# A two-layer trunk on one core: modulation vectors, block sums and the ends of its two MLPs

## The chip, the cores and the metric

The kernel runs on one core of one Trainium2 chip. The metric is the device time of one execution in microseconds (us). Before the change three runs gave 3522.86, 3525.76 and 3529.64 us; the median is 3525.76 us.

## The reference, cut to what matters

The reference is one inference step of a trunk with two layers. Each layer is a mixer followed by an MLP, both between RMS norms, with shift, scale and gate vectors that come from a conditioning vector. The change touches only the MLPs and the modulation vectors:

```python
def sq_relu_mlp(h, w_up, w_down):
    return jnp.square(jax.nn.relu(h @ w_up)) @ w_down
...
    for l in range(DEPTH):
        sh1p, sc1p, g1p, sh2p, sc2p, g2p = modulation(c_ctx[None, :], w_ada[l], b_ada[l])
        sh1s, sc1s, g1s, sh2s, sc2s, g2s = modulation(c, w_ada[l], b_ada[l])
        ...                                   # mixer of the layer: yp, ys
        xp = xp + g1p * rmsnorm(yp, norm_g[l, 1])
        xs = xs + g1s * rmsnorm(ys, norm_g[l, 1])
        hp = rmsnorm(xp, norm_g[l, 2]) * (1.0 + sc2p) + sh2p
        hs = rmsnorm(xs, norm_g[l, 2]) * (1.0 + sc2s) + sh2s
        xp = xp + g2p * rmsnorm(sq_relu_mlp(hp, w_up[l], w_down[l]), norm_g[l, 3])
        xs = xs + g2s * rmsnorm(sq_relu_mlp(hs, w_up[l], w_down[l]), norm_g[l, 3])
```

There are ten tiles of 128 rows, 1024 columns wide; the MLP goes up to 4096 columns and back. One modulation vector, written (l, j) here, is a product of two conditioning rows with a 1024 x 1024 block of w_ada.

## The kernel before, in words

All products are float32 in effect: each operand is split into a high and a low part (split: a cast on ScalarE, L198, and a subtraction on VectorE, L199), and each product is three matmuls (L193 to L195). Engine names are those of the profile: PE is TensorE, DVE is VectorE, ACT is ScalarE, POOL is GpSimd, SP is SyncE, which here issues loads in the order of its queue.

`mlp` runs twice, for layers 0 and 1. Its **up part** goes over 16 column blocks p. The first two are plain products. The other 14 use a block scheme with seven products instead of eight, for which sums of blocks of the weights are needed (s1 to s4, four additions on POOL, L543 to L546, in `units`) and the products are combined on DVE (L593, L614, L619 to L625). Then `close_x` rectifies and squares (L464 on ACT, L466 on DVE), forms four sums of hidden blocks (L469 to L479) and stores seven pieces in DRAM by POOL's queue (L462). A scheduler orders these instructions.

The **down part** is written out in order (manual_schedule). It goes over seven names of products, (1, 5, 6, 7, 4, 2, 3), eight pairs k each, 56 in all; a pair is 30 matmuls into five PSUM banks. While pair k is multiplied, `make` splits the operands of pair k + 2, and SP loads the hidden pieces of pair k + 5 into tiles sa and sb. After eight pairs `take` moves the five banks out. Row tiles that are finished go through `close`: sum of squares on ACT (L898), rsqrt on POOL (L204), multiply by rsqrt and gate G (L912) and add x (L913) on DVE, then for the next stage another square, another rsqrt, and a scaling (L927). `closes` advances three of these generators by turns. After the first MLP the next mixer follows: `modulate` transposes the tiles (tp) and four `kv_product` stages multiply them into PSUM (mmo).

`ada_steps` makes a modulation vector, in one of two ways. On PE, w_ada is the operand of 32-row matmuls (L265). On DVE (acc), pieces of 128 x 256 are multiplied by the conditioning values and summed (L287, L289), the sum is transposed and reduced into adaR (L295, L296), and small matmuls (adac, L300) fold the four blocks. Loads are issued in the step that uses them (L248). The first MLP's up part makes (0,5), (1,0) and (1,1), its down part (1,2), (1,3) and (1,4), one step after each pair from k = 2; the second MLP's up part makes (1,5). All seven are made on DVE before the change.

Of the kernel before, what the change touches and what calls it, by code (L numbers as in the profile page):

```python
# [9 lines left out]
F32 = mybir.dt.float32  # L10
# [100 lines left out]
class Net:  # L111
# [122 lines left out]

    def ada_steps(self, l, j, raw, pp, ptag="mm", pbufs=None, acc=None):

# [39 lines left out]
        if acc:  # L276
            R = self.const.tile([P, 4, KD, 2], F32, tag="adaR", name="adaR")
        for n in range(4 if acc else 0):
            y = acc().rearrange("p (s f) -> p s f", s=2)
            k = 0  # L280
            while k < KD:
                for k, w in load(k, n * 256, 256):
                    for s in range(2):
                        c = self.cs[:, k, s:s + 1]
                        E = nc.gpsimd if s in AE else nc.vector
                        if k == 0:
                            E.tensor_scalar(y[:, s], w, c, None, ALU.mult)  # L287
                        else:
                            E.scalar_tensor_tensor(y[:, s], w, c, y[:, s], ALU.mult, ALU.add)  # L289
                k += 1  # L290
                if k % AY == 0 and (k < KD or AZ):
                    yield
            for s in range(2):
                z = raw()[:, 0:256]
                nc.vector.transpose(z, y[:, s])  # L295
                nc.vector.tensor_reduce(R[:, :, 2 * n:2 * n + 2, s].rearrange("p b k -> p k b"), z.rearrange("p (k b c) -> p k b c", k=2, b=4), AX.X, ALU.add)  # L296
        if acc:
# [79 lines left out]
    def mlp(self, l, h, stage, late, fills, odd=None):  # L377
# [30 lines left out]
        def make(k):  # L408

            m, v = divmod(k, 8)  # L410
            n = names[m]
            tag = (("hh1", "hl1", "hh0")[k % 3]) if m < LASTP else ("hh1", "hl1")[k % 2]
# [39 lines left out]
        with self.pool("mu", 1) as up:  # L452
# [8 lines left out]
            def close_x(p, X):  # L461
                store = lambda i, z: nc.gpsimd.dma_start(hd[p, i], z)  # L462
                for c in range(2):
                    nc.scalar.activation(X[0, c], X[0, c], AF.Square)  # L464
                for c in range(2):
                    V.scalar_tensor_tensor(X[1, c], X[1, c], 0.0, X[1, c], ALU.max, ALU.mult)  # L466
                store(2, X[0, 1])
# [65 lines left out]
            def units():  # L533
                ring = cycle([(i, q) for i in range(3) for q in "hl"][:5])
                load_up(NS)
                for p in range(NS, NP):
                    a11, a21 = [raws[p][0][:, :, c * P:(c + 1) * P] for c in range(2)]
                    a12, a22 = [raws[p][1][:, :, c * P:(c + 1) * P] for c in range(2)]
                    s = [self.slot(3, q, F32).rearrange("p (i k f) -> p i k f", i=2, k=4) for q in "hl"]
                    s1, s2, s3, s4 = [s[i // 2][:, i % 2] for i in range(4)]  # L540
                    for j, u in enumerate((a11, a12, a21, a22, s4, s2, s3, s1)):
                        if j == 1:
                            Gp.tensor_tensor(s1, a21, a22, add)  # L543
                            Gp.tensor_tensor(s2, s1, a11, sub)
                            Gp.tensor_tensor(s4, a12, s2, sub)
                            Gp.tensor_tensor(s3, a11, a21, sub)  # L546
                        if j == 5 and p + 1 < NP:
# [26 lines left out]
            araw = cycle("hl")  # L574
            steps = (_ for f in fills[0] for _ in self.ada_steps(*f, lambda: self.slot(4, next(araw), F32), pp, "tp", None, lambda: self.slot(2, "l", F32)[:, :512]))
            T1, T2, T3 = [[T[i, k] for k in range(4)] for i in (1, 2, 3)]
# [62 lines left out]
        with self.pool("my") as yp, self.pool("md") as dp, self.tc.manual_schedule(engines=IN_ORDER):  # L639
# [12 lines left out]
            at = {5: (0, 1), 6: (1, 1), 3: (1, 1)}  # L652

            def traw():
                if flow:
# [8 lines left out]
            with ExitStack() as es:  # L664
# [3 lines left out]
                def mul(k, whole=None):  # L668
# [12 lines left out]
                    if whole is not None:  # L681
                        self.gemm(bank[m, whole], L(whole), lambda u: Tu[u], range(2), False, True)
                        return
# [21 lines left out]

                def pair(k):
                    m, v = divmod(k, 8)
                    mul(k)
                    if k + 2 < NK:
# [8 lines left out]
                with self.pool("mu2") as u2:  # L718
                    U = [u2.tile([P, 512], F32, name=f"u2{i}") for i in range(5)]
                    steps = (_ for f in fills[1] for _ in self.ada_steps(*f, lambda: self.act.tile([P, 256], F32, tag="hl2", name="ada_w"), pd, "b", 8, lambda: u2.tile([P, 512], F32, tag="ada_y", name="ada_y")))  # L720
# [4 lines left out]
                    for _ in steps:  # L725
                        pass
                with self.pool("ms", 2) as sp:
                    tmp = lambda: sp.tile([P, 512], F32, tag="tmp", name="tmp", bufs=3)
                    st = lambda: sp.tile([P, 512], F32, tag="st", name="kvw_raw", bufs=2)
# [18 lines left out]
                    for k in range(32, NK - 1):  # L748
                        pair(k)
                        if k == 41:  # L750
                            G.extend(self.slot(6, q, F32) for q in "hl")
                            self.load_G(l, 1, G)
                        closes(k - 43, 0, 5)
                        if k > 49:
                            go(M0, 2)
                        if k > 51:
                            go(wt)
                    for i in range(5):
                        mul(NK - 1, i)
                        take(LASTP, i)  # L760
                        closes(5 + i, 5, 10)
                        if i == 0:
                            go(M0, 8)
                            go(wt)
                    es.close()
                    self.open[self.ps_at] = self.pool("ps", 2, psum=True)
                    pp = self.pp = self.open[self.ps_at].__enter__()
                    if odd:
                        M2 = self.modulate(2, z, nxt, out, tmp, pp)
                        go(wt)  # L770
                        odd.kv_product(0)
# [7 lines left out]
                    else:  # L779
                        closes(10, 5, 10)  # L780
                        closes(11, 5, 10)
                    for it in f:
# [102 lines left out]
    def load_x(self, stage, ts, xs):  # L885
        for t, x in zip(ts, xs):
            self.nc.sync.dma_start(x, self.x_in(stage, t))

    def close(self, ts, y, mid, z, zt, stage, G, xs, late, sp, junk, nxt, padd=()):
# [1628 lines left out]
def build(ctx, tc, a, o, k):  # L2518
# [6 lines left out]
    d = Odd(net)  # L2525
    h, late = net.mlp(0, h, 1, late, (((0, 5), (1, 0), (1, 1)), ((1, 2), (1, 3), (1, 4))), d)
    d.run(late)
# [31 lines left out]
```

## Time and profile before

| | |
|---|---|
| median of three runs | 3525.76 us |
| profiled execution, its own time | 3527.33 us |
| its span | 3525.2 us |
| mean granted clock of TensorE | 0.967 |
| busy share of PE, DVE, ACT, POOL | 92%, 66%, 44%, 22% |
| DMA over the span | 123 GB/s |

The profiled execution is a further run; its span goes from its first to its last instruction. Busy shares are means over stages that differ, so the stages are looked at one by one: the first MLP's up part ends at about 1345 us with its down part from there to about 1808 us; the second MLP's up part runs to about 3150 us and its down part from there to the end. PEclk is the clock that was granted to TensorE as a share of full speed.

### The profile page before, as it was taken

The numbers are of one execution on the slowest core, as the hardware profiler recorded it, in microseconds if no ns is written. First come the engines' busy times: TensorE is split into PE (matmuls) and PEld (weight loads), VectorE is DVE, ScalarE is ACT, GpSimd is POOL, SyncE is SP. The second block draws the span as 40 slices with busy tenths as digits, with TensorE's granted clock in tenths as the row PEclk, the third lists the DMA queues.
The fourth block names the chain that finished last, engine by engine and source line by source line (L and its number), as shares of the span: only waits on it lengthen the run. The fifth ranks groups of instructions, "written<-read, shape, count | busy, mean of one in ns | idle before, by whom it ended". The sixth has DMA issues, their size and how long they took to land. (4 is left out here: it accounts for less than half of the span.)

```text
span 3525.2 us, 50186 instructions
## 1 busy us (share of the span) xinstructions
PE 3255.6 (92%) x17957; PEld 2657.2 (75%) x17957; DVE 2326.5 (66%) x4310; ACT 1555.8 (44%) x3697; POOL 758.7 (22%) x1084
## 2 busy tenths in 40 slices
PE   7899898979989999788979999999999899999997
PEld 4788778858877788666758876666678788888886
DVE  4666766663699967887555365666655986666665
ACT  4444544443533333323455456555555333344443
POOL 2323332321133330001211033000001333310112
PEclk9999999989999999999989999999999999999999
DMA  6333343273344536554432221000143343455444
GB/s 208 79 101 110 98 134 96 81 216 123 107 152 167 185 137 219 175 176 143 155 118 63 78 73 34 4 8 8 35 157 118 122 170 118 149 185 174 149 141 168
DMA packets 329959, 435.27 MB, mean 123 GB/s; under 512 B 30157, under 2 KB 231213, under 8 KB 329709
## 3 DMA queue, kind: packets, MB, share of 16 engines
q1 hardware_dynamic: 307116, 343.18, 31.6%
q0 software_dynamic: 22592, 88.89, 6.7%
q8 instruction: 141, 2.31, 0.3%
q14 instruction: 110, 0.89, 0.1%
HBM read 309.55 MB, written 122.43 MB: 123 GB/s over the span
## 5 line engine op out<-in xcount | busy, mean ns | idle before, releaser
L193 PE MATMUL y<-oph 128*128 128x512 f32 x896 | 352.3, 393 | 14.3 <-ACT y L694 4.9
L194 PE MATMUL y<-opl,oph 128*128 128x512 f32 x896 | 351.7, 393 | 0.0
L195 PE MATMUL y<-oph,opl 128*128 128x512 f32 x896 | 351.6, 392 | 0.0
L199 DVE TENSOR_TENSOR opl<-sa,oph 128x512 fp32r<-128x512 f32 x216 | 158.8, 735 | 202.7 <-ACT oph L198 202.4
L198 ACT CAST oph<-sa 128x512 fp32r<-128x512 f32 x216 | 133.7, 619 | 252.2 <-PE y L194 186.1
L193 PEld LDWEIGHTS y<-oph 128*128 128x128 f32 x896 | 170.3, 190 | 51.6 <-ACT y L694 5.4
L194 PEld LDWEIGHTS y<-opl,oph 128*128 128x128 f32 x896 | 170.1, 190 | 35.8
L195 PEld LDWEIGHTS y<-oph,opl 128*128 128x128 f32 x896 | 170.0, 190 | 35.6
L193 PE MATMUL mmf<-hh,wf_hi 128*128 128x512 f32 (+1 forms) x384 | 152.6, 397 | 0.0
L1007 DVE SCALAR_TENSOR_TENSOR u<-pre,cw,u 128x510 f32<-128x510 f32 (+2 forms) x192 | 144.1, 759 | 9.7 <-ACT u L1005 8.5
L462 POOL DMA_DIRECT2D hd<-x x96 | 52.6, 548 | 452.7 <-ACT x L464 296.3
L193 PE MATMUL mmt<-wt_hi,hh 128*128 128x256 f32 x480 | 148.9, 310 | 0.0
L204 POOL TENSOR_SCALAR rs_v<-ss 128x1 f32<-128x1 f32 x90 | 27.7, 307 | 540.7 <-ACT junk L898 392.7
L195 PE MATMUL mmf<-hh,wf_lo 128*128 128x512 f32 (+1 forms) x384 | 139.9, 364 | 0.0
L194 PE MATMUL mmf<-hl,wf_hi 128*128 128x512 f32 (+1 forms) x384 | 139.4, 363 | 0.0
L194 PE MATMUL mmt<-wt_lo,hh 128*128 128x256 f32 x480 | 136.8, 285 | 0.0
L195 PE MATMUL mmt<-wt_hi,hl 128*128 128x256 f32 x480 | 136.8, 285 | 0.0
L193 PE MATMUL o<-wh,hh 128*128 128x512 f32 x280 | 113.1, 404 | 0.0
L195 PE MATMUL o<-wh,hl 128*128 128x512 f32 x280 | 110.5, 395 | 0.0
L194 PE MATMUL o<-wl,hh 128*128 128x512 f32 x280 | 110.1, 393 | 0.0
L1935 PE MATMUL pom<-PTm,mla_h 128*64 128x256 f32 x336 | 106.5, 402 | 2.4 <-DVE ob L1947 2.0
L1935 PE MATMUL pom<-PTm,mla_l 128*64 128x256 f32 x336 | 107.0, 403 | 0.0
(1064 smaller groups left out, 10368.4 us busy)
## 6 DMA issues: line engine op xcount, KB each, us to landing
sa<-hd SPq DMA_DIRECT2D x108, 512.0 KB
hd<-s POOLq DMA_DIRECT2D x128, 320.0 KB, 2.6
hd<-x POOLq DMA_DIRECT2D x96, 320.0 KB, 2.7
wh<-in_w_down SPq DMA_DIRECT2D x40, 512.0 KB
wl<-in_w_down SPq DMA_DIRECT2D x40, 512.0 KB
w_raw<-in_w_ada SPq DMA_DIRECT2D x32, 512.0 KB
wh<-in_w_up SPq DMA_DIRECT2D x30, 512.0 KB
wl<-in_w_up SPq DMA_DIRECT2D x30, 512.0 KB
```

The lines of the kernel that those rows point to most:

```text
L193: mm(ps, lh, rh, start=first and j == 0, stop=False)
L194: mm(ps, lh, rl, start=False, stop=False)
L195: mm(ps, ll, rh, start=False, stop=last and j == n - 1)
L198: self.nc.scalar.copy(hi, raw)
L199: self.nc.vector.tensor_tensor(lo, raw, hi.bitcast(F32), ALU.subtract)
L204: nc.gpsimd.tensor_scalar(v, ss, scale, eps, ALU.mult, ALU.add)
L462: store = lambda i, z: nc.gpsimd.dma_start(hd[p, i], z)
L1007: nc.vector.scalar_tensor_tensor(us, pre[:, i:i + e - a], cw[:, b, j + i:j + i + 1], us, ALU.mult, ALU.add)
L1935: self.nc.tensor.matmul(self.po[64 * b:64 * b + 64, 0], self.odd.Vm[(0 if self.big else 10) + 2 * i + b][:, 64 * self.h:64 * self.h + 64], ...
```

## The change: what it does

In `ada_steps` a vector folded on DVE now loads its pieces a given number of steps ahead (`ahead`), has a step of its own before the last reduction's matmul and one more after it, and takes the tile of the transpose from a ring named by the caller (`turn`). In the up parts the pieces are 512 columns wide instead of 256. The block sums of the weights go from POOL to DVE, between the splits. `close_x` rectifies and squares on ACT alone. In the first MLP's down part only (1,2) and (1,3) are folded, at a rate that `pace` gives; (1,4) is made on PE in `more`, between the kv products after the MLP. `closes` goes through its tiles in the other order. In the second MLP the last two row blocks of the last product are multiplied bank by bank, and five tiles end in a new generator, `close_last`.

```diff
         if acc:
             R = self.const.tile([P, 4, KD, 2], F32, tag="adaR", name="adaR")
-        for n in range(4 if acc else 0):
-            y = acc().rearrange("p (s f) -> p s f", s=2)
...
+            y = acc()
+            f = y.shape[1] // 2
+            todo, got = [(n, k) for n in range(D // f) for k in range(KD)], []
+            def fetch(c):
+                while len(got) <= c and todo:
+                    n, k = todo[0]
+                    ws = load(k, n * f, f)
+                    del todo[:len(ws)]
+                    got.extend(ws)
...
+                for k in range(KD):
+                    fetch(c + 2 * ahead - 1 if c % 2 == 0 else c)
+                    w = got[c][1]
...
+                    if c % 2 == 0:
+                        fetch(c + 2 * ahead - 1)
+                        yield
+                m = f // P
+                for s in range(2):
+                    z = turn()[:, :f]
+                    nc.vector.transpose(z, y[:, s])
+                    nc.vector.tensor_reduce(R[:, :, m * n:m * n + m, s].rearrange("p b k -> p k b"), ...)
+                yield
+            yield
...
                 for c in range(2):
-                    V.scalar_tensor_tensor(X[1, c], X[1, c], 0.0, X[1, c], ALU.max, ALU.mult)
+                    nc.scalar.activation(X[1, c], X[1, c], AF.Square)
...
+                    adds = {0: (s1, a21, a22, add), 1: (s2, s1, a11, sub), 2: (s4, a12, s2, sub), 3: (s3, a11, a21, sub)}
                     for j, u in enumerate((a11, a12, a21, a22, s4, s2, s3, s1)):
-                        if j == 1:
-                            Gp.tensor_tensor(s1, a21, a22, add)
...
+                        if j in adds:
+                            V.tensor_tensor(*adds[j])
...
+            pace = lambda k: (2, *[int(k % 8 in (0, 2, 3, 5, 6))] * 4, 2 * (k < 44), 0)[k // 8]
...
                     for k in range(32):
                         pair(k)
-                        if k > 1:
-                            next(steps, None)
+                        go(steps, pace(k))
...
+                    if last:
+                        for n, t in enumerate(H[0]):
+                            x = (2, "h"), (2, "l"), (3, "h"), (3, "l"), (0, "h")
+                            f[5 + n] = self.close_last(t, y[t], G, lambda n=n: self.slot(*x[n], F32), stage, sp, junk, tmp)
                     def closes(w, lo, hi):
-                        for n in (w - 2, w - 1, w):
+                        for n in (w, w - 1, w - 2):
...
+                    ends = [NK - 2, NK - 1] if last else [NK - 1]
...
                     for i in range(5):
-                        mul(NK - 1, i)
+                        for k in ends:
+                            mul(k, i)
                         take(LASTP, i)
+                        if last:
+                            go(f[5 + i])
+                            if i:
+                                go(f[4 + i])
+                            continue
                         closes(5 + i, 5, 10)
                         if i == 0:
                             go(M0, 8)
-                            go(wt)
+                        go(wt)
...
+                        more = (_ for f in fills[2] for _ in self.ada_steps(*f, st, pp, "tp"))
...
                         odd.kv_product(1)
                         go(M2, 4)
                         closes(11, 5, 10)
+                        go(more, 5)
                         odd.kv_product(2)
+                        go(more, 5)
                         odd.kv_product(3)
...
+                        go(more, 9)
...
+    def close_last(self, t, y, G, x, stage, sp, junk, tmp):
...
+        nc.scalar.activation(junk()[:, :512], h[0], AF.Square, accum_out=ss[:, 0:1])
+        V.tensor_tensor(h[0], h[0], g[0], ALU.mult)
+        yield
...
+        r = self.rsqrt(sp, ss[:, 0:1], 1, 1.0 / D)
+        for q, a in zip(self.halves(x), (h[0], u)):
+            V.scalar_tensor_tensor(q, a, r, q, ALU.mult, ALU.add)
+        nc.sync.dma_start(self.x_out(stage, t), x)
```

The order of instructions shows three places.

On DVE, where the first MLP's last product is taken out of its banks, before the change (y4 to y9 are row tiles, xr tiles of x, wl6 and wh6 the gates):

```order
L704 TENSOR_TENSOR y4_13313<-y4_13313,y3_16726 128x512
L912 SCALAR_TENSOR_TENSOR y9_13312<-y9_13312,rs_r_17220,wl6_16310 128x1024
L913 TENSOR_TENSOR xr_17215<-y9_13312,xr_17215 128x1024
L704 TENSOR_TENSOR y5_13314<-y5_13314,y3_16727 128x512
L927 TENSOR_SCALAR y9_13312<-xr_17215,rs_r_17257 128x1024
L912 SCALAR_TENSOR_TENSOR y4_13313<-y4_13313,rs_r_17246,wh6_16309 128x1024
L913 TENSOR_TENSOR xr_17241<-y4_13313,xr_17241 128x1024
L704 TENSOR_TENSOR y6_13315<-y6_13315,y3_16728 128x512
```

The same place after the change:

```order
L724 TENSOR_TENSOR y4_13203<-y4_13203,y3_16452 128x512
L970 SCALAR_TENSOR_TENSOR y9_13202<-y9_13202,rs_r_16946,wl6_16020 128x1024
L971 TENSOR_TENSOR xr_16941<-y9_13202,xr_16941 128x1024
L199 TENSOR_TENSOR wl1_16976<-xr_16930,wh1_16975 128x2x416
L724 TENSOR_TENSOR y5_13204<-y5_13204,y3_16453 128x512
L970 SCALAR_TENSOR_TENSOR y4_13203<-y4_13203,rs_r_16968,wh6_16019 128x1024
L971 TENSOR_TENSOR xr_16963<-y4_13203,xr_16963 128x1024
L985 TENSOR_SCALAR y9_13202<-xr_16941,rs_r_17000 128x1024
L724 TENSOR_TENSOR y6_13205<-y6_13205,y3_16454 128x512
```

The scaling of a tile (L927, now L985) stood ahead of the next tile's multiply and add and stands behind them now; the last split of the mixer's weights (L199, wl1) has moved in between.

On PE, where the third kv product begins, before the change (tp are transposes, mmo the kv product; the first block of the product is shown):

```order
L195 MATMUL mmo<-wh_17333,hl_7_16929 128x416
...
L332 MATMUL tp<-ident,y_13317 128x128
L332 MATMUL tp<-ident,y_13312 128x128
L193 MATMUL mmo<-wh_17160,hh_0_16914 128x416
L194 MATMUL mmo<-wl_17161,hh_0_16914 128x416
```

The same place after the change, through the start of the fourth:

```order
L349 MATMUL tp<-ident,y_13207 128x128
L349 MATMUL tp<-ident,y_13202 128x128
L265 MATMUL ada_17202<-kvw_raw,cs 32x512 x8
L193 MATMUL mmo<-wh_16886,hh_0_16640 128x416
...
L195 MATMUL mmo<-wh_16975,hl_7_16655 128x416
L274 MATMUL adac<-selc,kvw_raw 128x2 x4
L265 MATMUL ada_17261<-kvw_raw,cs 32x512 x8
L193 MATMUL mmo<-wh_16886,hh_0_16640 128x416
```

Eight matmuls of vector (1,4) now stand ahead of each of the last two kv products, with their loads behind them in SP's queue.

On DVE in the first MLP's up part the additions that POOL made (L543 to L546) are new; after the change a stretch reads (L303 is the fold, L564 the block sums):

```order
L564 TENSOR_TENSOR wh3_10553<-wh5_10461,wl5_10463 128x512
L303 SCALAR_TENSOR_TENSOR wl2_10363<-wh4_10538,cs_92,wl2_10363 128x512
L564 TENSOR_TENSOR wh3_10553<-wh3_10553,wh5_10461 128x512
L303 SCALAR_TENSOR_TENSOR wl2_10363<-wh4_10538,cs_92,wl2_10363 128x512 x2
L199 TENSOR_TENSOR wh2_10556<-wh5_10461,wh2_10556 128x512
L303 SCALAR_TENSOR_TENSOR wl2_10363<-wh4_10538,cs_92,wl2_10363 128x512
L303 SCALAR_TENSOR_TENSOR wl2_10363<-wl4_10593,cs_92,wl2_10363 128x512 x2
L199 TENSOR_TENSOR wh0_10573<-wl5_10463,wh0_10573 128x512
```

The sums stand singly between folds and splits.

## Rows read from the trace of the kernel before

**Rows 1.** The page, part 1: busy time, share of the span, instructions.

```profile
PE 3255.6 (92%) x17957; PEld 2657.2 (75%) x17957; DVE 2326.5 (66%) x4310; ACT 1555.8 (44%) x3697; POOL 758.7 (22%) x1084
```

**Rows 2.** Table of stretches: window, us, busy PE, PEld, DVE, ACT, POOL, PEclk, DMA, GB/s.

```profile
985.00:1286.00 301.00, 280.56 (x1448) 236.44 (x1449) 269.57 (x470) 100.28 (x188) 105.38 (x120) 0.98 0.47 166
1375.00:1650.00 275.00, 225.86 (x967) 183.35 (x966) 223.20 (x435) 85.12 (x169) 26.17 (x20) 0.91 0.51 158
2730.00:2860.00 130.00, 115.42 (x603) 98.08 (x602) 118.83 (x198) 42.70 (x83) 42.87 (x44) 0.95 0.41 143
2900.00:3100.00 200.00, 200.00 (x1054) 170.91 (x1053) 124.92 (x168) 71.07 (x136) 71.15 (x88) 1.00 0.37 133
3150.00:3490.00 340.00, 340.00 (x1502) 281.53 (x1501) 215.60 (x313) 140.33 (x270) 46.76 (x35) 1.00 0.51 160
1808.00:1859.00 51.00, 26.25 (x114) 23.75 (x114) 25.34 (x53) 21.43 (x50) 9.90 (x24) 0.73 0.31 108
```

**Rows 3.** Waits of PE, 1345 to 1660 us: total us, times, longest.

```profile
PE adac L300 <- DVE adaR L296: 37.4, 3, 15.0
```

**Rows 4.** Waits of PE, 940 to 1345 us.

```profile
PE p L193 <- DVE x L619: 10.7, 6, 3.9
```

**Rows 5.** Waits of PE, 1660 to 1900 us.

```profile
PE mmo L193 <- ACT wh L198: 11.9, 1, 11.9
```

**Rows 6.** Timeline of DVE, 1815 to 1826 us: start, us, instruction, [idle before, releaser].

```profile
1816.40 0.68 DVE L704 TENSOR_TENSOR y<-y,y 128x512 f32<-128x512 f32 x1
1820.63 0.76 DVE L927 TENSOR_SCALAR wh<-xr,rs_r 128x1024 f32<-128x1024 f32 x1 [3.55 <-POOL rs_r L205]
1821.30 1.28 DVE L912 SCALAR_TENSOR_TENSOR y<-y,rs_r,wh 128x1024 f32<-128x1024 f32 x1
1822.62 1.23 DVE L913 TENSOR_TENSOR xr<-y,xr 128x1024 f32<-128x1024 f32 x1
1823.76 0.68 DVE L704 TENSOR_TENSOR y<-y,y 128x512 f32<-128x512 f32 x1
```

**Rows 7.** Timeline of PE and DVE, the end of the span.

```profile
3506.88 0.39 PE L195 MATMUL y<-oph,opl 128*128 128x512 f32 x1
...
3519.43 1.23 DVE L913 TENSOR_TENSOR xr<-y,xr 128x1024 f32<-128x1024 f32 x1 [0.79 <-DMA xr<-xres]
```

**Rows 8.** The chain that ended last, in order of time: start, us, what.

```profile
1898.02 3.75 DMA w_raw<-in_w_in_odd
...
3514.04 5.31 DMA xr<-xres
```

**Rows 9.** Timeline of DVE, 1014 to 1046 us.

```profile
1034.09 0.68 DVE L621 TENSOR_TENSOR x<-x,p 128x512 f32<-128x512 f32 x1
1034.69 0.69 DVE L199 TENSOR_TENSOR wl<-wh,wl 128x512 fp32r<-128x512 f32 x1
```

**Rows 10.** Groups on DVE by form, 2932 to 3082.5 us: busy, mean ns, idle before.

```profile
L199 DVE TENSOR_TENSOR wh<-wh,wh 128x512 fp32r<-128x512 f32 x13 | 14.2, 1092 | 9.4 <-ACT wh L198 8.8
L199 DVE TENSOR_TENSOR wl<-wh,wl 128x512 fp32r<-128x512 f32 x11 | 11.7, 1065 | 9.1 <-ACT wl L198 8.8
L199 DVE TENSOR_TENSOR wh<-wl,wh 128x512 fp32r<-128x512 f32 x16 | 11.0, 690 | 10.4 <-ACT wh L198 10.4
L466 DVE SCALAR_TENSOR_TENSOR x<-x 128x640 f32<-128x640 f32 x12 | 9.3, 819 | 0.0
```

**Rows 11.** Groups on DVE by form, 985 to 1239 us.

```profile
L289 DVE SCALAR_TENSOR_TENSOR wl<-wh,cs,wl 128x256 f32<-128x256 f32 x82 | 42.2, 578 | 0.0
```

**Rows 12.** Timeline of SP's queue and DVE, 1384 to 1398 us.

```profile
1384.73 3.78 SPq L248 DMA_DIRECT2D ada_w<-in_w_ada  x8
...
1388.77 0.62 DVE L287 TENSOR_SCALAR ada_y<-ada_w,cs 128x256 f32<-128x256 f32 x2 [2.86 <-DMA ada_w<-in_w_ada]
...
1394.42 3.25 DVE L289 SCALAR_TENSOR_TENSOR ada_y<-ada_w,cs,ada_y 128x256 f32<-128x256 f32 x8
```

**Rows 13.** Instructions of L265: duration in ns, minimum/median/maximum.

```profile
L265 PE MATMUL ada<-w_raw,cs x128: 592/617/1063, 7.7 to 785.5; 128*32 128x512 f32 x128
```

More of the change, by code (lines that the diff above doesn't have):

```diff
@@ L233, in ada, with ada_steps @@
             pass
-    def ada_steps(self, l, j, raw, pp, ptag="mm", pbufs=None, acc=None):
+    def ada_steps(self, l, j, raw, pp, ptag="mm", pbufs=None, acc=None, turn=None, ahead=1):
         nc = self.nc
@@ L277, in ada_steps @@
             R = self.const.tile([P, 4, KD, 2], F32, tag="adaR", name="adaR")
-        for n in range(4 if acc else 0):
-            y = acc().rearrange("p (s f) -> p s f", s=2)
-            k = 0
-            while k < KD:
-                for k, w in load(k, n * 256, 256):
+        if acc:
+            y = acc()
[7 more added lines that the diff above has]
+                    got.extend(ws)
+            c = 0
+            for n in range(D // f):
+                y = (acc() if n else y).rearrange("p (s f) -> p s f", s=2)
+                for k in range(KD):
+                    fetch(c + 2 * ahead - 1 if c % 2 == 0 else c)
+                    w = got[c][1]
+                    got[c] = None
+                    c += 1
@@ L283, in ada_steps @@
                     for s in range(2):
-                        c = self.cs[:, k, s:s + 1]
-                        E = nc.gpsimd if s in AE else nc.vector
+                        v = self.cs[:, k, s:s + 1]
                         if k == 0:
-                            E.tensor_scalar(y[:, s], w, c, None, ALU.mult)
+                            nc.vector.tensor_scalar(y[:, s], w, v, None, ALU.mult)
                         else:
-                            E.scalar_tensor_tensor(y[:, s], w, c, y[:, s], ALU.mult, ALU.add)
@@ L290, in ada_steps @@
[L290 to L296, printed above, removed]
+                            nc.vector.scalar_tensor_tensor(y[:, s], w, v, y[:, s], ALU.mult, ALU.add)
+                    if c % 2 == 0:
+                        fetch(c + 2 * ahead - 1)
+                        yield
@@ L297, in ada_steps @@
+                m = f // P
+                for s in range(2):
+                    z = turn()[:, :f]
+                    nc.vector.transpose(z, y[:, s])
+                    nc.vector.tensor_reduce(R[:, :, m * n:m * n + m, s].rearrange("p b k -> p k b"), z.rearrange("p (k b c) -> p k b c", k=m, b=4), AX.X, ALU.add)
+                yield
+            yield
         if acc:
@@ L411, in make @@
             n = names[m]
-            tag = (("hh1", "hl1", "hh0")[k % 3]) if m < LASTP else ("hh1", "hl1")[k % 2]
+            tag = (("hh1", "hl1", "hh0")[k % 3]) if m < LASTP or last else ("hh1", "hl1")[k % 2]
             t = lambda name: self.act.tile([P, 512], F32R, tag=tag, name=name)
@@ L574, in mlp @@
             araw = cycle("hl")
-            steps = (_ for f in fills[0] for _ in self.ada_steps(*f, lambda: self.slot(4, next(araw), F32), pp, "tp", None, lambda: self.slot(2, "l", F32)[:, :512]))
+            steps = (_ for f in fills[0] for _ in self.ada_steps(*f, lambda: self.slot(4, next(araw), F32), pp, "tp", None, lambda: self.slot(2, "l", F32), lambda: sx()[:, :512], 1))
             T1, T2, T3 = [[T[i, k] for k in range(4)] for i in (1, 2, 3)]
@@ L704, in take, with pair @@
                         V.tensor_tensor(z, z, ps, add)
-                def pair(k):
+                def pair(k, skip=False):
                     m, v = divmod(k, 8)
-                    mul(k)
+                    if not skip:
+                        mul(k)
                     if k + 2 < NK:
@@ L747, in mlp @@
                         wt = odd.kv_weights(self.order, lambda i: [self.slot(4, "hl"[i], F32)] if i < 2 else [st(), st()] if i < 3 else [xr()])
-                    for k in range(32, NK - 1):
+                    ends = [NK - 2, NK - 1] if last else [NK - 1]
+                    for k in range(32, ends[0]):
                         pair(k)
+                        go(steps, pace(k))
+                        if k == 44:
+                            go(steps, 99)
                         if k == 41:
@@ L887, in load_x @@
             self.nc.sync.dma_start(x, self.x_in(stage, t))
+    def close_last(self, t, y, G, x, stage, sp, junk, tmp):
+        nc, V = self.nc, self.nc.vector
+        h, g = self.halves(y), self.halves(G[t // 8])
+        ss = sp.tile([P, 2], F32, tag="ssl", name="ssl", bufs=5)
+        x = x()
+        self.load_x(stage, (t,), (x,))
+        nc.scalar.activation(junk()[:, :512], h[0], AF.Square, accum_out=ss[:, 0:1])
+        V.tensor_tensor(h[0], h[0], g[0], ALU.mult)
+        yield
+        nc.scalar.activation(junk()[:, :512], h[1], AF.Square, accum_out=ss[:, 1:2])
+        u = tmp()
+        V.tensor_tensor(u, h[1], g[1], ALU.mult)
+        yield
+        nc.gpsimd.tensor_tensor(ss[:, 0:1], ss[:, 0:1], ss[:, 1:2], ALU.add)
+        r = self.rsqrt(sp, ss[:, 0:1], 1, 1.0 / D)
+        for q, a in zip(self.halves(x), (h[0], u)):
+            V.scalar_tensor_tensor(q, a, r, q, ALU.mult, ALU.add)
+        nc.sync.dma_start(self.x_out(stage, t), x)
+        yield
     def close(self, ts, y, mid, z, zt, stage, G, xs, late, sp, junk, nxt, padd=()):
```

23 lines of the change are left out of this document (11 added, 12 removed).

## The prediction

> **What bounds the kernel now.** I read the page first: TensorE (PE) is busy 92% of the span, no other engine over 66% [rows 1]. So a microsecond counts only where PE stands still or runs at its lower clock, and the change works inside the two MLPs. I then asked for their stretches [rows 2]. Two need no help: the up part of the second MLP once its modulation vector is done (2900 to 3100 us: PE busy throughout, 1054 matmuls in 200 us, 5.27 a us) and its down part (1502 in 340 us, 4.42 a us). Against these rates the stretches in which modulation vectors are folded on VectorE (DVE) fall behind: 985 to 1286 us makes 1448 matmuls, worth 274.8 us, so 26.2 are lost; 1375 to 1650 makes 967, worth 218.9, so 56.1 are lost; 2730 to 2860 makes 603, worth 114.4, so 15.6 are lost. In all three DVE is busy 81 to 91%, in the clean ones 62 and 63%. The waits name the same culprit: in the first MLP's down part PE waits 37.4 us in only three places, for the last block reduction (adaR, L296) before the small matmul adac, which stands in PE's queue close behind it [rows 3]; in the up part it waits for DVE's sums [rows 4]. Then the two ends. From 1808 to 1859 us PE does 114 matmuls with its clock at 0.73 [rows 2]; 11.9 us of that is one wait for a weight cast [rows 5]. And 17.9 us lie between the last matmul (3506.88 + 0.39 [rows 7]) and the end of the span.
>
> **Up parts (block sums to DVE, rectify and square to ACT, wider and prefetched folds).** One pass p over a column block is 132 matmuls, 25.0 us at 5.27 a us. In the clean stretch DVE needs 124.92 / 200 x 25.0 = 15.6 us of it [rows 2]. Added: four sums; a 128x512 tensor_tensor follows the one before it by 0.60 us [rows 9], so 2.4 us. Removed: two 128x640 operations of L466, 9.3 us for 12 [rows 10], so 1.55. A third part is not in the diff: the splits that fall beside POOL's sums take 1092 and 1065 ns, the others 690 [rows 10]. In six passes 24 of 48 are slow ones, 4 a pass, and 4 x 0.39 = 1.6 us goes if POOL's arithmetic goes. Net -0.7: 14.9 us. A fold step was eight operations of 128x256 at 42.2 / 82 = 0.51 us [rows 11], and a transpose and a reduce that I count like two more: 5.1 us, 15.4 for three steps a pass, with the base 31.0 us of 25.0. Now a step is four operations of 128x512, priced at 0.60 like the sums, and less than one transpose or reduce: 4.7 x 0.60 = 2.8, three of them 8.5 a pass, 23.4 of 25.0 us with the base. DVE just keeps up. ACT takes four operations a pass for the two that DVE loses; at the 0.78 us of those it gains 3 us on a busy share of 71.07 / 200 = 36% [rows 2]: hidden. I leave 5 us of the 26.2 and 3.5 of the 15.6, since the folds' transposes now take tiles from the ring of the stored sums and so wait for stores: gains 21 and 12. Bounds: nothing gained to all of it, 0 to 42 together.
>
> **Down part of the first MLP.** A pair k is 30 matmuls, 6.8 us. DVE's own work in it is four splits at 0.60 and a half-width one, mostly with two subtractions: 2.7 to 3.9 us. Eight fold operations take 3.25 us [rows 12], the fold's transposes and reduces, counted alike, 0.8: 6.7 to 8.0 us for the pair's 6.8; on top DVE waits for loads that are issued only when they are needed (2.86 us [rows 12]). So DVE runs late and the three adac matmuls pay. After: one of the three vectors leaves, loads run three steps ahead, and pace sets two half-size steps a pair for k < 8 (2.7 + 3.25 + 0.7 = 6.7 us, level with PE), then five in eight pairs (3.9 + 1.2 = 5.1 us), so DVE is on time; and two empty steps stand between the last reduction and adac. The 37.4 us go, and with them the clock's fall to 0.91 [rows 2]. What is late next is the first eight pairs and the takes of full banks; I leave 8 of 56.1: gain 48. Bounds: 10 (waits stay, clock and takes improve) to 56.
>
> **End of the first MLP.** Two edits of opposite sign. Reordered closes: DVE now does multiply and add of the tile one back before it scales the tile two back. Before, a round was add, two squares on ACT, two rsqrts on POOL, scale and multiply in series, and takes are 7.4 us apart (1816.40 and 1823.76 [rows 6]). Now the longest work on one engine is take 0.68 + multiply 1.28 + add 1.23 + scale 0.76 = 3.95 us a round, unless the x loads (5.31 us for 512 KB [rows 8]) hold it. kv product 0 starts after the fourth take: some 5 us after the last matmul instead of 9 (1816.40 + 0.68 against 1808); the last weights' cast stands before the closes, so the 11.9 us go too. Against it: vector (1,4) now runs on PE here, 16 matmuls at 0.617 us [rows 13] = 9.9 us, their weights in 16 loads of 256 KB through two tiles. PE is in order: a load from the third on waits for the matmul that frees its tile, and kv products 2 and 3 stand behind them. A weight load of the next stage took 3.75 us [rows 8], so two tiles cost 3.75 + 0.62 + 0.1 = 4.5 us; three such rounds in the first half, four in the second. After the last matmul: kv 0 at +5, about 6 us (half clock at first), transposes that wait for ACT, kv 1 to +19.5, transposes to +22, first half to +38 (three small loads stand ahead in the queue), kv 2 to +44, second half to +61, kv 3 to +67. Before, the stage took 51 us. So it costs 15. Bounds: loads hidden, all PE work in a row (5 + four products at 4.6 + 5 + 9.9 = +38), a gain of 13; no overlap at all (14 x 4.4 + 35 = +97), a cost of 45. I keep 15, from the 3.75 us row.
>
> The Trainium skill ("DMA: Bandwidth & Descriptors", Anatomy of one DMA) fits a transfer of the gpsimd path as 2.0 us and its bytes at 436 GB/s: an estimate of 2.6 us for 256 KB, by which the seven rounds would be 8 us shorter and the sum 8 us lower. No row here shows a lone 256 KB load on SP's queue.
>
> **End of the kernel.** The last two row blocks of the last product are now multiplied bank by bank, the first half of each tile is squared and scaled before that, and x is loaded early, so the 5.31 us wait for it [rows 8] goes. What stays after the last matmul: take 0.68, multiply and add in one pass of 1.28 [rows 6], landing 4.5 (3525.2 less 3519.43 + 1.23 [rows 7]); between them half a square, its sum and rsqrt, which I bound by 2 and 5 us and put at 3.5: 10 of 17.9. Gain 8, bounds 6 and 9.5.
>
> **Sum.** 21 + 48 + 12 + 8 - 15 = 74. The profiled execution took 3527.33 us (span 3525.2), 1.6 more than the median of 3525.76: 3527.3 - 74 = 3453, as a median 3452 us.
>
> **Rivals.**
> 1. DVE stays the bound in the up parts: the sums' time is not given back by quicker splits. For it: DVE is 90% busy from 985 to 1286. Against: the slow splits [rows 10]. The gains 21 and 12 go, and 0.9 us in each of 11 folding passes comes on top: 3452 + 33 + 10 = 3495. The Trainium skill ("Perfetto Trace Analysis", Optimizing Scalar/DVE Operations) advises the opposite move, off DVE when it is saturated, GpSimd included, though it doubts that it helps between these two; the slow splits bear out the doubt. Chance 0.10.
> 2. The PE vector is hidden: loads land during the kv products and the quicker closes show in full, +38 instead of +67: 3452 - 28 = 3424. For it: DMA is 31% busy there [rows 2]. Against: two tiles only. 0.12.
> 3. The adac waits stay, since DVE is still late at k < 8 and after: 3452 + 37 = 3489. 0.06.
> 4. Slower: SP's queue. SP's loads go out in order; a fold's load waits until DVE has used its tile, and the loads sa of later pairs stand behind it. If DVE falls over three pairs (20 us) back, sa's lead is used up, and each of 32 pairs with a step runs step 1.9, load 5.3, cast 0.6, splits 3.4 in series: 11.2 for 6.8 us, 141 us in place of the gain of 48: 3452 + 48 + 141 = 3641. Before, eight fold loads at once already stood there (3.78 us of issue [rows 12]) without that. 0.04.
>
> **How the numbers follow.** The forecast holds 0.65, the rivals 0.32, anything else 0.03. Range 3424 to 3490: the likeliest case alone (3430 to 3475), rivals 2 and 3; it leaves out 1, 4 and the far bound of the end. About 0.2% (7 us) is what a measurement of this kernel can tell from no change: faster 0.94, same 0.02, slower 0.04.
>
> **What would show it.** Right: no wait of PE for adaR over 1 us; over 5.1 matmuls a us in the first up part; splits beside the sums at 0.69 us; takes of the first MLP's last product about 4 us apart; PE waiting 20 to 30 us for L265's loads between the kv products; the last matmul 10 us before the end. Wrong: DVE over 95% busy in the up parts, sa's loads late, or PE waits at L265 under 10 us.

## The result and the profile after

The changed kernel took 3443.56 us (median of four runs, 3439.49 to 3445.69), the kernel before 3524.31 beside it: a ratio of 0.9767, 95% interval 0.975 to 0.9784. The forecast was 3452. The profiled execution has a span of 3441.7 us, 83.5 less than before. Part 1 of its page, as [rows 1]:

```profile
PE 3250.1 (94%) x17997; PEld 2645.0 (77%) x17997; DVE 2236.0 (65%) x4130; ACT 1635.7 (48%) x3829; POOL 603.7 (18%) x977
```

The stretches after, with the columns of [rows 2]: first MLP's up part, its down part, the kv products after it, second MLP's up part.

```profile
982.00:1263.00 281.00, 275.20 (x1441) 233.58 (x1440) 241.30 (x383) 126.91 (x233) 41.21 (x77) 0.99 0.52 175
1351.00:1531.00 180.00, 180.00 (x802) 148.72 (x801) 148.40 (x272) 73.42 (x141) 11.60 (x10) 1.00 0.63 194
...
1733.00:1797.00 64.00, 46.79 (x157) 26.91 (x157) 14.22 (x22) 14.71 (x31) 7.52 (x14) 0.74 0.38 119
2668.00:2784.00 116.00, 111.21 (x598) 95.23 (x597) 100.63 (x160) 51.94 (x98) 15.68 (x29) 1.00 0.48 163
```

The up part now makes 1441 matmuls in 281 us, 5.13 a us, where [rows 2] had 4.81; the second stretch has no gap. The waits of PE, from 912 to 1333 us and from 1333 to 1690 us, the longest of each, answer to [rows 3, 4]; adaR is not among them:

```profile
PE p L193 <- DVE x L637: 4.1, 5, 1.6
```

```profile
PE y L193 <- DVE y L724: 1.7, 1, 1.7
```

At the first MLP's end (1690 to 1800 us) the wait of [rows 5] is gone and one for the loads of vector (1,4) is new. The wait of kv product 0 for its take stays:

```profile
PE ada L265 <- DMA kvw_raw<-in_w_ada: 12.7, 9, 2.8
PE mmo L193 <- DVE y L724: 10.2, 1, 10.2
```

In the kernel before (1660 to 1900 us) it was:

```profile
PE mmo L193 <- DVE y L704: 9.2, 1, 9.2
```

The timeline of PE shows the first half of vector (1,4). Each row is four records, two for each of L265's f32 matmuls (the code issues 16, the trace has 32 records):

```profile
1751.72 1.65 PE L265 MATMUL ada<-kvw_raw,cs 128*32 128x512 f32 x4 [0.47 <-ACT tmp L355]
1756.16 2.61 PE L265 MATMUL ada<-kvw_raw,cs 128*32 128x512 f32 x4 [2.79 <-DMA kvw_raw<-in_w_ada]
1760.88 2.54 PE L265 MATMUL ada<-kvw_raw,cs 128*32 128x512 f32 x4 [2.10 <-DMA kvw_raw<-in_w_ada]
1765.62 2.50 PE L265 MATMUL ada<-kvw_raw,cs 128*32 128x512 f32 x4 [2.21 <-DMA kvw_raw<-in_w_ada]
```

On DVE the takes (L724) of the last product, [rows 6] before, stand 5.3 to 6.1 us apart; a weight split and a wait for rsqrt lie between them:

```profile
1720.59 0.68 DVE L724 TENSOR_TENSOR y<-y,y 128x512 f32<-128x512 f32 x1
1721.19 1.28 DVE L970 SCALAR_TENSOR_TENSOR y<-y,rs_r,wl 128x1024 f32<-128x1024 f32 x1
...
1725.77 1.03 DVE L199 TENSOR_TENSOR wl<-xr,wh 128x832 fp32r<-128x832 f32 x1 [2.05 <-ACT wh L198]
1726.71 0.68 DVE L724 TENSOR_TENSOR y<-y,y 128x512 f32<-128x512 f32 x1
...
1731.35 0.75 DVE L985 TENSOR_SCALAR y<-xr,rs_r 128x1024 f32<-128x1024 f32 x1 [1.50 <-POOL rs_r L205]
1732.02 0.68 DVE L724 TENSOR_TENSOR y<-y,y 128x512 f32<-128x512 f32 x1
```

The end of the span, [rows 7] before: 11.3 us lie behind the last matmul (3441.7 less 3429.99 + 0.39), not 17.9. L943 is the multiply and add of `close_last`.

```profile
3429.99 0.39 PE L195 MATMUL y<-oph,opl 128*128 128x512 f32 x1
...
3434.54 0.74 DVE L943 SCALAR_TENSOR_TENSOR wh<-tmp,rs_r,wh 128x512 f32<-128x512 f32 x1
```

The table gives all kernels by stage, in us. The stages are cut by names of tiles, in each kernel's one profile: at the first matmul of ups (the plain products of an up part), of y (the banks of a down part) and of qaps (the product behind the kv products), and at the last of y; "end 0" runs from the first MLP's last matmul to qaps, behind the kv products. Not shown: the mixer between (727 to 730) and the second down part (381 in all).

| kernel | median | ratio to before | start | up 0 | down 0 | end 0 | up 1 | end 1 |
|---|---|---|---|---|---|---|---|---|
| before | 3524.31 | | 907.8 | 447.0 | 453.3 | 159.3 | 431.8 | 18.0 |
| changed | 3443.56 | 0.975-0.9784 | 912.3 | 420.9 | 389.5 | 180.5 | 417.6 | 11.4 |
| c0 | 3432.65 | 0.9737-0.9767 | 898.1 | 421.5 | 389.4 | 179.9 | 418.0 | 11.4 |
| e1 | 3462.58 | 0.9815-0.9846 | 905.9 | 434.4 | 389.4 | 179.8 | 428.5 | 11.4 |
| e2 | 3434.77 | 0.9738-0.9774 | 903.0 | 426.5 | 389.4 | 179.8 | 420.8 | 11.4 |
| e3 | 3407.24 | 0.9647-0.9688 | 906.4 | 423.0 | 394.5 | 146.4 | 418.2 | 11.4 |
| e4 | 3399.82 | 0.9635-0.967 | 906.2 | 420.1 | 389.4 | 146.4 | 417.6 | 11.4 |
| e5 | 3403.06 | 0.9657-0.9686 | 905.0 | 421.1 | 395.5 | 147.3 | 418.7 | 11.3 |
| e6 | 3413.08 | 0.9658-0.9715 | 901.9 | 423.7 | 402.0 | 143.1 | 419.4 | 11.4 |
| e9 | 3399.93 | 0.9645-0.9674 | 896.5 | 422.9 | 389.4 | 148.3 | 418.0 | 11.4 |
| e10 | 3406.41 | 0.9646-0.9683 | 905.0 | 423.9 | 394.8 | 146.6 | 418.0 | 11.4 |
| e11 | 3406.11 | 0.9657-0.9686 | 904.9 | 419.2 | 396.9 | 146.0 | 418.4 | 11.4 |
| e12 | 3409.78 | 0.9669-0.9704 | 901.6 | 424.2 | 393.2 | 153.7 | 416.4 | 11.4 |
| e13 | 3406.87 | 0.9659-0.9689 | 907.7 | 422.9 | 389.4 | 150.6 | 417.5 | 11.4 |

### The profile page after: what moved, and what is told of

Read it like the earlier page. It is cut to its first block, busy times and chain, and to the rows that moved or that the text cites. A ratio compares the mean times of both kernels' runs of the same rounds, so it can differ in the third digit from the quotient of the medians.

```text
span 3441.7 us, 50028 instructions
## 1 busy us (share of the span) xinstructions
PE 3250.1 (94%) x17997; PEld 2645.0 (77%) x17997; DVE 2236.0 (65%) x4130; ACT 1635.7 (48%) x3829; POOL 603.7 (18%) x977
## 5 line engine op out<-in xcount | busy, mean ns | idle before, releaser
L199 DVE TENSOR_TENSOR opl<-sa,oph 128x512 fp32r<-128x512 f32 x216 | 158.8, 735 | 167.2 <-ACT oph L198 166.9
L405 ACT ACTIVATE x<-x 128x512 f32<-128x512 f32 x112 | 70.3, 628 | 78.7 <-DVE x L638 60.5
```

The source lines that it names most:

```text
L199: self.nc.vector.tensor_tensor(lo, raw, hi.bitcast(F32), ALU.subtract)
L405: relu = lambda o, i: nc.scalar.activation(o, i, AF.Relu)
```

## The experiments

**c0, the changed kernel again.**

> The changed kernel once more, as the mark for the others of this batch. The stage ahead of the first MLP, whose code is the same in all kernels, took 907.8 us in the profile of before and 912.3 in that of after, but 903.0 to 906.4 in the three variants; if that is chance, it comes out near 906 here, and the time at 3437 to 3443 us. Rival: the change itself makes that stage longer (912 again).

The rival is out: the start came out at 898.1 us, and over all profiles of the same code it lies between 896.5 and 912.3. It scatters more than I expected, and the time came out lower than I expected. Between two batches the medians of this one kernel differ by 10.9 us, so small effects are read from the stages. These scatter too: the seven kernels with one and the same first up part (changed, c0, e3, e5, e6, e10, e11) took 419.2 to 423.9 us for it; the first down part, where its code is the changed kernel's, took 389.4 or 389.5 each time.

**e1, block sums on POOL.**

```diff
-                        if j in adds:
-                            V.tensor_tensor(*adds[j])
+                        if j == 1:
+                            Gp.tensor_tensor(s1, a21, a22, add)
...
```

> The changed kernel with the weights' block sums back on POOL, all else as changed. My theory: moving the sums is nearly free either way, because what DVE gives up in sums (four operations of about 0.6 us a pass) it gets back as slower splits beside POOL's arithmetic (about 4 x 0.39 us a pass): time within 5 us of the changed kernel's 3443.6, and the splits beside the sums at 1.07 to 1.09 us instead of 0.69. Rival: POOL's arithmetic also slows the folds beside it, so that the up parts fall behind again: 10 to 20 us lost in the first MLP's up part and 5 or more in the second's, 3458 to 3470 us.

My theory fell and the rival came, in its stages and in the time: 13 us are lost in the first up part and 10.5 in the second (against c0). Matched matmul by matmul with the changed kernel, 11 of the first 13 are lost between 965 and 1035 us, where folding begins and DVE is behind. DVE there, by form, of this kernel and then of the changed one (mean ns behind the busy time):

```profile
L303 DVE SCALAR_TENSOR_TENSOR wl<-wh,cs,wl 128x512 f32<-128x512 f32 x11 | 11.0, 1024 | 0.0
...
L489 DVE TENSOR_TENSOR s<-x 128x640 f32<-128x640 f32 x3 | 3.6, 1185 | 0.0
```

```profile
L303 DVE SCALAR_TENSOR_TENSOR wl<-wh,cs,wl 128x512 f32<-128x512 f32 x8 | 5.7, 748 | 0.0
...
L489 DVE TENSOR_TENSOR s<-x 128x640 f32<-128x640 f32 x3 | 2.5, 819 | 0.0
```

Folds and other sums slow beside POOL's arithmetic as well, not the splits alone. The means mix operations beside an addition with others. In e1's timeline a fold beside an addition of POOL's took 1.77 us, the next one without an addition 0.74:

```profile
964.87 1.73 POOL L566 TENSOR_TENSOR wl<-wh 128x512 f32<-128x512 f32 x1
```

```profile
965.38 1.77 DVE L303 SCALAR_TENSOR_TENSOR wl<-wl,cs,wl 128x512 f32<-128x512 f32 x1
...
968.91 0.74 DVE L303 SCALAR_TENSOR_TENSOR wl<-wl,cs,wl 128x512 f32<-128x512 f32 x1
```

The Trainium skill ("SBUF — State Buffer", SBUF: two separate sides) says that a DVE operation with two SBUF inputs and a GpSimd operation that reads SBUF share a port pair that one holds while the other waits; these rows agree.

**e2, narrow folds in the up parts.**

```diff
-... lambda: self.slot(2, "l", F32), lambda: sx()[:, :512], 1))
+... lambda: self.slot(2, "l", F32)[:, :512], lambda: sx()[:, :512], 1))
...
-                    if c % 2 == 0:
+                    if c % (2 if ahead > 1 else 4) == 0:
```

> The changed kernel with pieces of 256 columns in the up parts as before (eight fold operations a step, one step per four rows' blocks as before), loads one step ahead and sums on DVE kept. My theory: the width is what brings DVE below PE in a folding pass; with 0.41 us an operation of 128x256 against 0.66 of 128x512 a pass costs DVE 2 to 3 us more plus two more transposes and reduces, and it is the bound again: 5 to 12 us lost over both up parts, 3449 to 3456 us. Rival: the gain in the up parts came from loads ahead and from POOL's arithmetic being gone, and the width does nothing: within 3 us of 3443.6.

By stages 5.0 and 2.8 us are lost against c0, within what I expected of the width. These are single profiles, and 426.5 and 420.8 lie only 2.6 and 1.4 us above the highest of the kernels with wide folds. The median, from another batch than c0, doesn't resolve it; it lies below the range that I gave, which was reckoned from 3443.6.

**e3, the third vector on DVE in the down part; e4, in the up part.** The build line's lists and, in e3, the pace:

```diff
-... (((0, 5), (1, 0), (1, 1)), ((1, 2), (1, 3)), ((1, 4),)), d)
+... (((0, 5), (1, 0), (1, 1)), ((1, 2), (1, 3), (1, 4)), ()), d)          # e3
+            pace = lambda k: (2 if k < 8 or k % 3 == 0 else 1) if k < 44 else 0
+... (((0, 5), (1, 0), (1, 1), (1, 4)), ((1, 2), (1, 3)), ()), d)          # e4
```

> The changed kernel with vector (1,4) folded on DVE in the first MLP's down part again, with the loads ahead and the steps spread over pairs 0 to 43 (two steps a pair for k below 8 and every third pair, else one), nothing of it on PE. After the last product the stage falls from 74 to about 40 us (34 us less). My theory: the loads ahead and the steps before the small matmul healed the down part, and DVE has room for the third vector (3.3 us of its own and 2.6 of folds in a pair of 6.8 us): the down part loses at most 8 us, 3410 to 3418 us. Rival: it was the missing vector that healed it: the down part loses 30 us or more, PE waits for adaR again, 3440 us or more.

> The changed kernel with vector (1,4) folded on DVE in the first MLP's up part as a fourth vector there, nothing of it on PE. 45 steps for 42 places, so that the last three passes are folding passes too and three steps are drained at the end. The stage after the last product falls by 34 us. My theory: with wide folds a folding pass is within 0.5 us of a clean one, so the up part loses 3 to 8 us: 3413 to 3418 us. Rival: DVE is the bound of folding passes and the drain adds a wait of PE: the up part loses 15 us or more, 3425 us or more.

Both rivals are out, and the forecasts were somewhat too slow: the third vector costs the down part 5.1 us and the up part nothing that the stages show, while end 0 falls by 33.5 us against c0. The 5.1 us are not lost while DVE folds: they are one wait for a take, at 1665.9 us, behind the last adac. PE's longest wait in e3's down part (1330 to 1690 us), where the changed kernel has 1.7:

```profile
PE y L193 <- DVE y L724: 5.9, 1, 5.9
```

In e4's profile PE waits from 1690 to 1800 us mainly for these (three more are 1.2 us or less):

```profile
PE mmo L193 <- DVE y L724: 10.2, 1, 10.2
PE tp L349 <- ACT tmp L355: 3.8, 4, 2.4
PE mmo L193 <- ACT wh L198: 1.9, 1, 1.9
```

So the vector on PE costs some 34 us, and e4 beats both kernels.

**e5, e10, e11, e6: what healed the down part.** All on e3. e5 loads one step ahead instead of three (the last argument), e10 in the step itself, e11 makes steps of eight operations, one a pair, e6 drops the two steps between the last reduction and adac:

```diff
+                    fetch(max(c + 1, c + 2 * ahead - 1) if c % 2 == 0 else c)      # e10, ahead = 0
+                    if c % (4 if f == 256 else 2) == 0:                            # e11, ahead = 2
+            pace = lambda k: int(1 < k < 44)                                       # e11
+                if n < D // f - 1 or ahead == 1:                                   # e6
+                    yield
+            if ahead == 1:
                 yield
-            yield
```

> The kernel with the third vector on DVE in the first MLP's down part, but loads one step ahead there, not three (the down part took 394.5 us with three). My theory: the loads ahead are what heals the down part; a step is 2 us of DVE and a load takes longer than one pair leaves for it when several stand in SP's queue, so DVE waits 1 to 3 us in many of the 63 steps and the down part takes 410 us or more. Rival: the even steps and the two steps before the small matmul heal it, one step ahead is enough: 392 to 398 us.

> The kernel with the third vector on DVE in the first MLP's down part, even steps as before this, but each step issues its own two loads when it begins, as the kernel before did (none ahead). One ahead gave 395.5 us for the down part, three 394.5. My theory: the first load ahead is what heals the part; in the kernel before DVE waited 27.0 us in 11 waits for those loads, and with 63 steps that issue their own loads DVE waits 1 to 2 us in most of them: 405 us or more. Rival: the size of a step heals it (four fold operations, not eight): 400 us or less even so.

> The kernel with the third vector on DVE, loads ahead (two pairs of pieces), two steps before the small matmul, but steps of eight fold operations, one after each pair for k from 2 to 43, as the kernel before had them. My theory: with the loads there, size matters little, since DVE has the same work in the same 44 pairs; 394 to 402 us for the down part. Rival: the lumps of 3.3 us and more make DVE late for the splits of the next pair: 410 us or more.

> The same kernel with the third vector on DVE, loads three ahead, but without the two steps between a vector's last reduction and its small matmul adac in the down part. My theory: DVE is on time now, so the small matmul waits only for DVE's lead: below 5 us for three vectors together, down part 393 to 400 us. Rival: the two steps are what takes the 37.4 us of waits away: PE waits 5 us or more for each of the three again, down part 410 us or more.

Against e3's 394.5 us, taking away loads ahead (395.5, 394.8) or the small steps (396.9) hardly matters, each by itself; my theories on both loads fell, that on size held. Without the empty steps 7.5 us are lost in the down part, between what I and the rival expected, and 3.3 of them come back in end 0. The loss is this wait of PE (1330 to 1690 us):

```profile
PE adac L319 <- DVE adaR L311: 9.1, 2, 5.0
```

What all of these share is that three vectors lie over 44 pairs, not over some 25. The stretches of the kernel before, in which it folds, and of e10, with the columns of [rows 2]:

```profile
1360.00:1500.00 140.00, 122.15 (x528) 99.22 (x528) 112.61 (x234) 46.11 (x92) 3.84 (x5) 0.95 0.59 179
1500.00:1604.00 104.00, 72.98 (x309) 58.87 (x307) 89.31 (x186) 27.37 (x55) 6.32 (x5) 0.86 0.54 170
```

```profile
1345.00:1480.00 135.00, 134.49 (x602) 111.04 (x601) 122.11 (x248) 54.18 (x107) 3.07 (x5) 1.00 0.66 207
1480.00:1600.00 120.00, 120.00 (x538) 99.09 (x537) 113.27 (x203) 48.09 (x96) 23.21 (x15) 1.00 0.55 179
```

Before, 837 matmuls are 27.9 pairs and DVE is busy 201.9 us: 7.2 a pair, and PE needs 6.7 (180 us for 802 / 30 pairs in the changed kernel). That is some 14 us of work too much. DVE's waits for the loads of the folds come on top, in the kernel before (1345 to 1660 us) and then in e10 (1330 to 1690 us):

```profile
DVE ada_y L287 <- DMA ada_w<-in_w_ada: 27.0, 11, 4.3
...
DVE ada_y L289 <- DMA ada_w<-in_w_ada: 1.9, 2, 1.5
```

```profile
DVE ada_y L301 <- DMA ada_w<-in_w_ada: 8.2, 4, 2.5
...
DVE ada_y L303 <- DMA ada_w<-in_w_ada: 1.3, 1, 1.3
```

With 28.9 us of them it is 8.3 a pair before, and DVE falls behind until PE waits for it at adac. In e10 it is 235.4 us for 38.0 pairs, 6.2 a pair, and below 6.5 with its waits, so that DVE keeps its lead. That the spread is the cause is argued, by leaving out the others one at a time and by this sum; it isn't shown by itself. By the sum the waits for loads were the larger part of the lag, and they are small in e10 too, where a step has two loads and not four. Two kernels would tell and were not tried: three vectors over 25 pairs with the rest as changed, and, over 44 pairs, steps of eight operations that issue their own loads.

**e9, takes first.** On e4:

```diff
-                        closes(5 + i, 5, 10)
+                        if i < 2:
+                            go(f[5 + i], 2)
...
+                        go(f[5], 2)
+                        go(f[6], 2)
+                        for w in (7, 8, 9):
+                            closes(w, 5, 10)
```

> The kernel with vector (1,4) in the up part, and at the first MLP's end all five takes of the last product ahead of DVE's closing work (only squares and rsqrts of the first two tiles start before). In the changed kernel the takes come 5.3 to 6.1 us apart with closing work, a weight split and a wait for rsqrt between them, and the first kv product waits 10.2 us for the fourth take. My theory: the takes then follow the products 1.4 us apart, kv product 0 starts 1 to 3 us after the last matmul, but the tiles it leaves are scaled later: 4 to 8 us less than 3399.8. Rival: the closing of tile 8 is the longest chain, and what kv product 0 gains the transposes lose: within 2 us of it, or more.

The rival won. kv product 0 starts 7 us earlier, 3.0 us after the last matmul, and the transposes of the tile that is scaled later lose it:

```profile
PE tp L349 <- ACT tmp L355: 7.2, 4, 6.0
PE tp L349 <- DVE y L991: 3.8, 1, 3.8
PE mmo L193 <- DVE y L724: 3.0, 1, 3.0
```

**e12, the old order of closes; e13, the weights' splits at their old place.** On e4:

```diff
-                        for n in (w, w - 1, w - 2):
+                        for n in (w - 2, w - 1, w):          # e12
...
-                        go(wt)
+                            go(wt)                           # e13, under "if i == 0"
```

> The kernel with vector (1,4) in the up part and closes in the old order (two back, one back, this one). From the last matmul of the first MLP to the first matmul behind the kv products it took 146.4 us, the kernel before 159.3, so the edits at this place other than the vector gave 12.9. My theory: the order of the closes gives the larger part: kv product 0 starts 5 to 8 us later, 152 to 156 us. Rival: the order gives nothing, 148 us or less, and it is the weights' casts that moved ahead.

> The kernel with vector (1,4) in the up part, closes in the new order, but the mixer's weights split where the kernel before split them (after the first bank of the last product and ahead of kv product 0), not after each bank. My theory: kv product 0 starts 2 to 4 us earlier, as no split stands between the takes, but then waits 8 to 12 us for the last weights' cast as before: 151 to 157 us for that stretch. Rival: the wait is gone for another reason (the closes): 148 us or less.

The stretch grows by 7.3 us in e12 and by 4.2 in e13, of 12.9 in all; e12 loses another 3.8 in the down part. In e12 it is not kv product 0 that is late, as I expected, but the transposes behind it, so that 153.7 us lies in my range by luck; in e13 kv product 0 starts 2.9 us earlier, but the cast is waited for again, 6.3 us in the middle of that product, and the clock stays lower (0.80 from 1705 to 1765 us, 0.89 in e4). e13 ends just below the range I gave. PE's waits from 1690 to 1760 us, e12 and then e13:

```profile
PE tp L349 <- ACT tmp L355: 10.8, 4, 9.7
PE mmo L193 <- DVE y L724: 9.8, 1, 9.8
```

```profile
PE mmo L193 <- DVE y L724: 7.3, 1, 7.3
PE mmo L193 <- ACT wh L198: 6.3, 1, 6.3
```

## Why the prediction was right, and where not

The sum was 74 us, measured in the two profiles 83.5, by the terms: 26.1 for 21 in the first up part, 63.8 for 48 in its down part, 14.2 for 12 in the second up part, 6.6 for 8 at the end, 21.2 lost for 15 at the first MLP's end; the start took 4.5 more and the mixer 1.6 more without a cause in the change. It is luck that the sum came so near: the 15.8 us by which the down part's term was too small are offset by 6.2 at the first MLP's end and 6.1 in stages that the change leaves alone. In detail:

- **Up parts.** The size was right; as much came back as was counted as lost, and none of PE's waits in the first up part is for a store. The signs came: 5.13 matmuls a us, DVE busy 86% (241.30 of 281 us), and splits of 681 to 689 ns on average (985 to 1265 us). The pass of 31.0 us of DVE was priced too high, though: [rows 2] have 269.57 us for 1448 matmuls, 24.6 for 132 on average, and 11 folding passes of 31.0 would have lost 66 us, not 26.2. The size came from the lost time, not from that sum. The step "the sums' time is given back by quicker splits" names the gain too narrowly: e1 shows that the move itself is worth 13 and 10.5 us, because folds and sums of DVE beside POOL's additions were slow as well, where DVE is behind. Rival 1 is out.
- **Down part.** The term was too small, 48 for 63.8, and above its bound of 56: the lost time was counted at 4.42 matmuls a us, the stretch then ran at 4.46, which makes 58. Matched matmul by matmul, 61.2 us came back in that stretch, since the count takes 24 small adac matmuls for whole ones, and 2.6 behind it. Of the four reasons the prediction gives, the vector that leaves and the loads ahead are not needed when the steps are spread (e3, e5, e10). The two empty steps are worth 7.5 us (e6); that the rest is pace is argued, as said above.
- **First MLP's end.** The sign was right, the size was 6 us short. For the vector on PE the prediction counts 33 us (+22 to +38 and +44 to +61), and 33.5 were measured, but by luck: two errors cancel. PE's 16 matmuls were put at 0.617 us each, but [rows 13] count two records a matmul, and here 21 of the 32 records run at 1.06 us, with the clock at 0.74 over the stretch: 20.7 us (9.3 and 11.4) instead of 9.9. In return a load is quicker than the 3.75 us taken from [rows 8]: PE waits 12.7 us for loads in all, not 20 to 30. So the rounds took 4.7 us against 4.5. The step that failed is the earlier start of kv product 0 by reordered closes, 5.2 of the 6 us. The takes came 5.3 to 6.1 us apart, not 4: the 3.95 us counted DVE's work alone, and left out the split and the rsqrt between. So kv product 0 waits 10.2 us, not 5, which is no less than the 9.2 before. What the order of the closes gave, 7.3 us, came at the transposes behind that product (e12).

SP issues the second round's loads as the first round ends, and the matmul of 1756.16 begins 2.8 us later:

```profile
1753.39 0.81 SPq L248 DMA_DIRECT2D kvw_raw<-in_w_ada  x2
```

The Trainium skill ("DMA: Bandwidth & Descriptors", Anatomy of one DMA) has a fit for the gpsimd path, by which 256 KB take an estimated 2.6 us; this load on SP's queue agrees with it. The row that I took instead is of a load of 512 KB, twice the size: the cast that waits for it in the kernel before reads 128x1024 f32.

```profile
1901.79 1.04 ACT L198 CAST wh<-w_raw 128x1024 fp32r<-128x1024 f32 x1 [0.22 <-DMA w_raw<-in_w_in_odd]
```

- **Hidden vector (rival 2).** It wasn't hidden. Hidden loads would have taken away the 12.7 us of waits for them (an estimate from that row), where the prediction had 28 for rival 2. The 33.5 us of e4 are more than that, since there the 20.7 us of matmuls go as well.
- **Kernel's end.** 6.6 for 8; the last matmul lies 11.3 us ahead of the end, for 10. Rivals 3 and 4 did not come: no wait for adaR, and no wait of PE in the down part is over 1.7 us.

## What to carry to other kernels

Where an engine works beside the bound one, compare its work in a unit of the loop, and its waits, with the bound one's time for it: 7.2 us of work and 1.0 of waits for loads against 6.7 went with a loss of some 60 us, 37.4 of them at three small matmuls. With the same work spread thinner (6.2) in small steps these waits went, without any prefetch. Work that is moved to the engine that bounds the kernel has to be paid in full where it stands; the same vector cost 34 us on PE and 0 to 5 on an engine that had room. And a change of many edits should be read stage by stage: here one edit of it lost 34 us of what the others gained.

## What the runs showed of the hardware

A matmul of L265 (512 columns, f32 operands that are not split) stands as two records in the trace: 592 to 617 ns each where the granted clock is 1.00 (1773 to 1781 us of the profile after), mostly 1.06 us where it is 0.50 (1752 to 1768 us). A fold of 128x512 on DVE took 0.74 us alone and 1.77 us beside an addition of POOL's (e1); the group averaged 1024 ns there and 748 ns in the changed kernel. And a stage whose code is the same in all fourteen profiles varied by 16 us: in the profile after, PE waited once 8.1 us for w_raw there, in the profile before 3.5 at most.
